# Two of the four output chunks of each attention output projection as Strassen products, in a two-layer decoder trunk on one core

## The chip, the core and the metric

The kernel runs on one core of one Trainium2 chip. The time is that of the device for one launch, in microseconds (us), as the median of several runs. TensorE (PE in the profile) does the matrix products, VectorE (DVE) and ScalarE (ACT) the work on single elements, GpSimd (POOL) a few masks, and SyncE (SP) issues nearly all transfers (DMA) between the chip's main memory and the core's on-chip memory.

## The reference

512 tokens of 2048 features pass two layers. Both layers end in the same way, and that end is what the change is about:

```python
def mixer(...):                      # attention of 16 heads of 128, sparse in layer 0, stick-breaking in layer 1
    return (o * jax.nn.silu(gate)) @ w_o            # output projection, 2048 x 2048

for i in range(DEPTH):                              # DEPTH = 2
    h = mixer(...)
    x = layer_norm(ALPHA * x + h, ln_g[i], ln_b[i]) # ALPHA = sqrt(2), over the 2048 features
    x = x + (p[i] @ w_ple[i]) * jax.nn.sigmoid(x @ w_ple_gate[i])
```

All is float32, and the outputs have to come out close to float32 accuracy.

## The kernel before

**Layout.** Activations lie with features on the 128 partitions and the 512 tokens along the free axis: a matrix of 2048 features is 16 blocks of 128 x 512. `F[0]` to `F[3]` (four blocks each, `fblock(n)` is block n) hold the running activations, `XH[k]` and `XL[k]` the two parts of block k when it is the operand of a projection.

**A product in three matmuls.** A float32 operand is split into a high part of reduced precision and the rest: `split` (L129) lets ACT write the high part and DVE the rest, so DVE always waits for ACT. `mm3` (L133) then issues three matmuls: high by high (L134), high weight by low activation (L135) and low weight by high activation (L136).

**Weights.** They are loaded as float32 in units of two row blocks (`raw`, three buffers, loaded by SP in the order of the list `units`), split into `wh` and `wl` (three buffers each, L224), and handed to TensorE two items ahead (`Ahead`, L203). An item is one row block of weights; its `wh` can be written only when TensorE is through with the item three before it. A plain product (`gemm_w`, L269) takes 16 items for a chunk of 512 output features, four `mm3` each, into four PSUM banks; with 256 features an item has two `mm3`.

**Strassen products.** Layer 1's shared keys, values and queries are already made this way (`strassen_items` L325, `gemm_s` L365, `combine` L388). A chunk of 512 output features becomes seven products of half the size in three dimensions: per item seven `mm3` on 256 tokens, 16 items to a chunk, into seven PSUM banks. On the side of the weights, DVE makes four sums `st` of each `raw` unit and splits them with ACT into `sh` and `sl` (three buffers each), beside `wh` and `wl` of 384 columns. On the side of the activations, `c3h` and `c3l` hold the split sums (`stream_sums`, L435), and the second half of the tokens in `XH[0..7]`, `XL[0..7]` is overwritten by one more sum, `t1` (`turn_first`, L448). `combine` puts a chunk together from its seven banks with three ACT copies and eight DVE sums.

**Order.** PE's order is the program's own order. ACT, DVE, POOL and SP each have one queue, in which instructions run strictly in order; a scheduler sets that order at build time. Side work (sums, squares, normalisation) stands in a list `bg` whose pieces `pumped` (L313) lets go between matmuls.

**The end of a layer** (`finish_layer`, L835). Before the change, all 2048 output features are plain products: three chunks of 512, then two of 256 (L892, L919). The residual is loaded over `F` by SP as soon as a part of `F` has been split (L901); DVE scales it and takes off a first estimate `cen` of the mean (`centred_residual`, L885), adds the projection out of PSUM (`onto`, L889), and gathers the sum `S` and the sum of squares `Qs` over the blocks (`moments`, L874). `total` (L857) sums over partitions with two matmuls: once in the second chunk, for `cen`, after nine items, and twice during `embed` (L965), the product of the per-layer embedding `p` that follows the projection. Before the last eight `mm3` steps, `pT` is loaded and split into `pth` and `ptl` (L947).

Of the kernel before, what the change touches and what calls it, by code (L numbers as in the profile page):

```python
# [10 lines left out]
F32 = mybir.dt.float32  # L11
# [66 lines left out]
def trunk_kernel(  # L78
# [42 lines left out]
    top = ctx.enter_context(tc.tile_pool(name="top", bufs=1))  # L121
    dram = ctx.enter_context(tc.tile_pool(name="dram", bufs=1, space=DRAM))
# [53 lines left out]

# [47 lines left out]
    def weight_parts():  # L224
        return tuple(top.tile([128, 512], F32R, name=n, tag=n, bufs=3) for n in ("wh", "wl"))
# [99 lines left out]
    def strassen_items(widths, wp):  # L325
        units = [n for n in widths for _ in range(NK // 2)]

        def prepare(n):
            raw = next_raw()
            rows = n // 256  # L330
            q = raw.rearrange("p a (b n) -> p (a b) n", b=2)
            two = [q[:, i].rearrange("p (j c) -> p j c", j=rows) for i in range(4)]
            st = wp.tile([128, 4 * H], F32, name="st", tag="st", bufs=2)[:, : 2 * n]
            st = st.rearrange("p (j i c) -> p j i c", j=rows, i=4)
            dve.tensor_tensor(st[:, :, 0], two[0], two[2], ALU.add)
            dve.tensor_tensor(st[:, :, 2], two[1], two[0], ALU.subtract)
            return q, two, st

        ready = prepare(units[0])
        for u, n in enumerate(units, 1):  # L340
            q, two, st = ready
            s1, s2, s3, s4 = (st[:, :, i] for i in range(4))
            dve.tensor_tensor(s2, s1, two[1], ALU.subtract)
            dve.tensor_tensor(s4, two[3], s2, ALU.subtract)
            rows = n // 256
            for j in range(rows):
                wh = top.tile([128, 512], F32R, name="wh", tag="wh", bufs=3)
                wl = top.tile([128, 512], F32R, name="wl", tag="wl", bufs=3)
                sh = wp.tile([128, 4, 128], F32R, name="sh", tag="sh", bufs=3)
                sl = wp.tile([128, 4, 128], F32R, name="sl", tag="sl", bufs=3)  # L350
                qh, ql = (w.rearrange("p (b c) -> p b c", b=4)[:, 0:3] for w in (wh, wl))
                split(qh, ql, q[:, 1:4, j * 128 : (j + 1) * 128])
                split(sh, sl, st[:, j])
                if j == rows - 1 and u < len(units):
                    ready = prepare(units[u])
                yield [(qh[:, i], ql[:, i]) for i in range(3)] + [(sh[:, i], sl[:, i]) for i in range(4)]

    def strassen_stream(widths, wp):
        return Ahead(strassen_items(widths, wp), 2)
# [28 lines left out]
    def combine(wp, M, dst):  # L388

        m1, m2, m6, m7, m5, m3, m4 = M  # L390
        u = wp.tile([128, 2, H], F32, name="u", tag="u", bufs=1)[:, : m1.shape[1]]
# [6 lines left out]
        dve.tensor_tensor(u, m6, u, ALU.add)  # L398
        pinned[0] = False

        def onto(c):
            dve.tensor_tensor(c, c, u, ALU.add)

        def rest():
            dve.tensor_tensor(c22, c12, c21, ALU.add)
            dve.tensor_tensor(c12, m3, c12, ALU.add)
            dve.tensor_tensor(c21, c21, m4, ALU.subtract)

        paced(rest)
        return [lambda c=c: onto(c) for c in (c12, c21, c22)]  # L410

    def combine_last(wp, M, dst):
# [6 lines left out]
        for out, a, b, op in (  # L419
            (c11, m2, u, ALU.add),  # L420
            (u, m6, u, ALU.add),
            (c21, m7, u, ALU.add),
            (c22, m5, c21, ALU.add),
            (c12, m5, u, ALU.add),
            (c12, m3, c12, ALU.add),
            (c21, c21, m4, ALU.subtract),
        ):
            dve.tensor_tensor(out, a, b, op)
# [19 lines left out]
    def turn_first(k, t1):  # L448

        split(XH[k][:, H:T], XL[k][:, H:T], t1)  # L450

# [45 lines left out]

    def add_finish(layer, w_o):
        add_parts(w_o, PARTS)
# [78 lines left out]
    iws = ip.tile([128, 3, 16], F32, name="iws")  # L578
    stacks = {}

    rc = ip.tile([128, 4], F32, name="rc")
    pool.dma_start(rc, rope_c)
# [750 lines left out]
```

## Time and profile before

| | |
|---|---|
| median of 3 runs | 1887.85 us (1887.64 to 1889.21) |
| span of the profiled execution | 1886.3 us |
| around it, against the median | 1.55 us |
| PE, DVE, ACT busy | 99%, 65%, 49% of the span |
| output projection of layer 0 | 620.5 to 795.6 us of the span |
| granted TensorE clock | full, in all slices |

A line of the page or of a view names the source line, the engine, the operation, and its tiles as out<-in; L111 is the helper through which nearly all ACT and DVE instructions are issued, so the tile names tell them apart. A matmul's row is longer than its share of the time, since matmuls overlap: the pace is the distance from one start to the next. The same holds, less strongly, for rows of DVE and ACT.

### The profile page before, as it was taken

What the parts mean: (1) busy time and instruction counts of PE and PEld (TensorE: products, weight loads), DVE (VectorE), ACT (ScalarE), POOL (GpSimd) and SP (SyncE); (2) the same over time, 40 slices, a digit from 0 to 9 for tenths busy, and PEclk for the clock granted to TensorE, in tenths of its full rate; (3) what the DMA queues carried; (4) which work ended last, traced back from release to release, by engine and by line L of the source; (5) the groups of instructions that cost most, each with busy time, mean ns of one, the idle gap of its engine ahead of it and who ended that gap; (6) DMA issues with size and microseconds to landing.
All of it is one profiled execution on the core that took longest, in us unless ns stands there. A gap on an engine that the chain in (4) does not pass through costs nothing.

```text
span 1886.3 us, 25050 instructions
## 1 busy us (share of the span) xinstructions
PE 1872.6 (99%) x9229; PEld 1586.7 (84%) x9229; DVE 1218.9 (65%) x2384; ACT 928.1 (49%) x1690; POOL 28.4 (2%) x49
## 2 busy tenths in 40 slices
PE   9999999999999999999999999999999999999998
PEld 8898888888888888888888999988888888888887
DVE  5668879966556454675368788866656645567534
ACT  4446323355554432474245444468877743347422
POOL 0000000000000000000000000000100000000000
PEclk9999999999999999999999999999999999999999
DMA  6432333312222432333343333322122153242333
GB/s 185 137 115 64 101 91 99 101 56 68 67 68 60 162 114 78 123 101 103 121 130 116 103 100 113 102 90 72 63 68 68 60 186 100 74 129 89 123 101 112
DMA packets 110587, 189.22 MB, mean 100 GB/s; under 512 B 8240, under 2 KB 28208, under 8 KB 110464
## 3 DMA queue, kind: packets, MB, share of 16 engines
q1 hardware_dynamic: 110320, 187.33, 32.4%
q8 instruction: 72, 1.18, 0.3%
q14 instruction: 51, 0.42, 0.1%
q0 software_dynamic: 144, 0.30, 0.1%
HBM read 179.21 MB, written 8.39 MB: 99 GB/s over the span
## 4 chain that ended last, share of the span: by engine, by line
PE 96%; DVE 2%; ACT 1%; DMA 1%; issue 0%; SPq 0%; POOL 0%; DVEq 0%; POOLq 0%
PE g L134 12%; PE g L135 12%; PE g L136 12%; PE o L135 7%; PE o L134 7%; PE o L136 7%; PE m L134 3%; PE m L135 3%; PE m L136 3%; PE q L136 3%; PE q L134 3%; PE q L135 3%; PE z L1214 2%; PE k L136 2%; PE k L135 2%; PE k L134 2%
## 5 line engine op out<-in xcount | busy, mean ns | idle before, releaser
L111 ACT ACTIVATE wh<-raw 128x512 fp32r<-128x512 f32 (+3 forms) x684 | 396.4, 581 | 674.4 <-PE g L135 239.4
L111 DVE TENSOR_TENSOR wl<-raw,wh 128x512 fp32r<-128x512 f32 (+3 forms) x684 | 429.6, 629 | 429.9 <-ACT wh L111 415.1
L134 PE MATMUL g<-xh,wh 128*128 128x512 f32 x1024 | 403.9, 394 | 0.2
L135 PE MATMUL g<-xl,wh 128*128 128x512 f32 x1024 | 400.3, 391 | 0.6 <-DVE xl L111 0.6
L136 PE MATMUL g<-xh,wl 128*128 128x512 f32 x1024 | 399.9, 390 | 0.0
L134 PEld LDWEIGHTS g<-xh,wh 128*128 128x128 f32 x1024 | 192.8, 188 | 40.4 <-ACT sg L111 1.9
L136 PEld LDWEIGHTS g<-xh,wl 128*128 128x128 f32 x1024 | 192.3, 188 | 40.8
L135 PEld LDWEIGHTS g<-xl,wh 128*128 128x128 f32 x1024 | 192.5, 188 | 38.4 <-DVE xl L111 1.4
L136 PE MATMUL o<-xh,wl 128*128 128x512 f32 x512 | 199.4, 389 | 0.1
L134 PE MATMUL o<-xh,wh 128*128 128x512 f32 x512 | 199.2, 389 | 0.0
L135 PE MATMUL o<-xl,wh 128*128 128x512 f32 x512 | 199.2, 389 | 0.0
L136 PEld LDWEIGHTS o<-xh,wl 128*128 128x128 f32 x512 | 96.1, 188 | 20.6 <-DVE wl L111 0.7
L134 PEld LDWEIGHTS o<-xh,wh 128*128 128x128 f32 x512 | 96.1, 188 | 20.2 <-ACT wh L111 0.2
L135 PEld LDWEIGHTS o<-xl,wh 128*128 128x128 f32 x512 | 96.1, 188 | 20.0
L134 PE MATMUL q<-xh,wh 128*128 128x512 f32 x256 | 99.6, 389 | 0.0
L135 PE MATMUL q<-xl,wh 128*128 128x512 f32 x256 | 99.6, 389 | 0.0
L136 PE MATMUL q<-xh,wl 128*128 128x512 f32 x256 | 99.6, 389 | 0.0
L111 ACT ACTIVATE sh<-st 128x512 fp32r<-128x512 f32 x80 | 49.0, 628 | 79.7 <-PE m L135 42.5
L111 DVE TENSOR_TENSOR sl<-st,sh 128x512 fp32r<-128x512 f32 x80 | 54.4, 689 | 37.2 <-ACT sh L111 37.2
L111 DVE TENSOR_TENSOR xl<-f,xh 128x512 fp32r<-128x512 f32 x80 | 54.3, 686 | 11.4 <-ACT f L111 11.0
L111 ACT ACTIVATE wk<-z 128x512 f32<-128x512 f32 x80 | 47.1, 590 | 25.7 <-PE z L136 18.0
L135 PEld LDWEIGHTS q<-xl,wh 128*128 128x128 f32 x256 | 48.1, 188 | 10.0
(290 smaller groups left out, 3366.5 us busy)
## 6 DMA issues: line engine op xcount, KB each, us to landing
raw<-w_in_a SPq DMA_DIRECT2D x95, 512.0 KB, 3.7
raw<-w_in_b SPq DMA_DIRECT2D x64, 512.0 KB, 3.8
raw<-w_ple_gate SPq DMA_DIRECT2D x52, 512.0 KB, 3.7
raw<-w_o_a SPq DMA_DIRECT2D x24, 512.0 KB, 3.9
raw<-w_o_b SPq DMA_DIRECT2D x24, 512.0 KB, 3.8
raw<-w_kv_b SPq DMA_DIRECT2D x16, 512.0 KB, 3.8
raw<-w_ple_gate SPq DMA_DIRECT2D x24, 256.0 KB, 2.9
f<-xT SPq DMA_DIRECT2D x4, 1024.0 KB, 6.4
```

The costliest lines, as they stand in the source:

```text
L111: ins = method(*args, **kw)
L134: pe.matmul(out, a[0], b[0], start=start, stop=False)
L135: pe.matmul(out, a[0], b[1], start=False, stop=False)
L136: pe.matmul(out, a[1], b[0], start=False, stop=stop)
L1214: pe.matmul(z, m, p, start=False, stop=n == len(terms), skip_group_check=True)
```

## The change

In both layers the output projection becomes: 512 features plain (here called stage A), 256 plain (B), chunks 2 and 3, that is blocks 8 to 15, as Strassen products (C2 and C3), and the remaining 256 features of chunk 1 plain (D). The embedding (E) follows as before.

- A and B use the rows of the activations in pairs (k, k + 8), and the four sums for Strassen are made beside them.
- The second token half of blocks 0 to 7, which `t1` overwrites, is stored to main memory before A (`late_halves`) and loaded and split again in D (`restore`).
- The attention output is scaled by 1/ALPHA where it is written, so the residual needs no factor; 1e-5 becomes 1e-5/ALPHA^2.
- ACT reads A's and B's banks out into `F`. The residual is then added by seven accumulating transfers that POOL issues (`add_residual`, 512 KB each), for 14 of the 16 blocks; for the last two it is loaded by SP and the projection is added by DVE.
- Taking off `cen` is one DVE instruction for two blocks (1024 elements a partition).
- `total` for `cen` stands after 11 items of B.
- Signs in the Strassen sums change for all Strassen products, with as many instructions as before. Some tiles get another size or place (`edge`, `iws`, `rc`, the descriptor memory).

PE has 9668 rows in the order after and 9092 before: 576 more, which is four chunks of 336 matmuls in place of four of 192.

Three places of the order, layer 0; layer 1 has the same rows. First, **ACT in the first chunk of 512**. Before, the high part `xh` of a block follows the `wh` of the item in front; `xh5` is used by item 5, and `wh_5649` is item 5's:

```order
L111 ACTIVATE wh_5631<-raw_5573 128x512
L111 ACTIVATE xh4_78<-f1_107 128x512
L111 ACTIVATE wh_5649<-raw_5573 128x512
L111 ACTIVATE xh5_79<-f1_107 128x512
L111 ACTIVATE wh_5670<-raw_5591 128x512
L111 ACTIVATE xh6_80<-f1_107 128x512
```

After, item 6 uses `xh3`, item 12 `xh6`; `wh_5723` is item 7's and `wh_5858` item 13's:

```order
L111 ACTIVATE wh_5707<-raw_5614 128x512
L111 ACTIVATE wh_5723<-raw_5614 128x512
L111 ACTIVATE c3h1_5568<-tf_5685 128x768
L111 ACTIVATE xh3_81<-f0_110 128x512
L111 ACTIVATE xh11_89<-f2_112 128x512
```

and, later in the same chunk:

```order
L111 ACTIVATE wh_5858<-raw_5750 128x512
L111 ACTIVATE xh7_85<-f1_111 128x512
L111 ACTIVATE xh15_93<-f3_113 128x512
L111 ACTIVATE c3h4_5574<-tf_5820 128x768
L111 ACTIVATE xh6_84<-f1_111 128x512
```

So the parts of one pair of blocks now stand behind a `wh` of a later item than the one that first uses them.

Second, **DVE ahead of the first `total`**, whose operand is `tl`. Before:

```order
L111 SCALAR_TENSOR_TENSOR f0_106<-f0_106,o0_5588 128x512
L111 TENSOR_TENSOR wl_5993<-raw_5900,wh_5992 128x512
L111 TENSOR_TENSOR S_5566<-S_5566,f0_106 128x512
L111 TENSOR_TENSOR tl_6062<-S_5566,th_6061 128x512
L111 TENSOR_TENSOR wl_6012<-raw_5936,wh_6011 128x512
```

After, with `wl_6079` item 11's, `wl_6093` item 12's and `wl_6113` item 13's; PE's first `total` matmul stands right behind item 10:

```order
L111 TENSOR_TENSOR S_5556<-f0_110 128x512
L111 TENSOR_TENSOR wl_6079<-raw_6013,wh_6078 128x256
L111 TENSOR_TENSOR xl1_95<-t11_5603,xh1_79 128x256
L111 TENSOR_TENSOR wl_6093<-raw_6041,wh_6092 128x256
L111 TENSOR_TENSOR S_5556<-S_5556,f0_110 128x512
L111 TENSOR_TENSOR xl2_96<-t12_5604,xh2_80 128x256
L111 TENSOR_TENSOR S_5556<-S_5556,f0_110 128x512
L111 TENSOR_TENSOR wl_6113<-raw_6041,wh_6112 128x256
L111 TENSOR_TENSOR st_6150<-raw_6090 128x256 x2
L111 TENSOR_TENSOR st_6150<-st_6150,raw_6090 128x256
L111 TENSOR_TENSOR tl_6107<-S_5556,th_6106 128x512
```

The three sums `S` now stand between the `wl` of items that come after `total`.

Third, **DVE at the end of the projection**. Before, the last weights are these (`wl_6854` and `wl_6864` belong to items 14 and 15 of the last 256 features):

```order
L111 TENSOR_TENSOR wl_6842<-raw_6785,wh_6841 128x256
L111 TENSOR_TENSOR ptl0_6876<-raw_6829,pth0_6875 128x512
L111 TENSOR_TENSOR ptl1_6880<-raw_6829,pth1_6879 128x512
L111 TENSOR_TENSOR wl_6854<-raw_6807,wh_6853 128x256
L111 TENSOR_TENSOR wl_6864<-raw_6807,wh_6863 128x256
```

After, from D's item 12 (`wl_7443`) to item 15 (`wl_7485`):

```order
L111 TENSOR_TENSOR wl_7443<-raw_7394,wh_7442 128x256
L111 TENSOR_TENSOR f3_113<-f3_113,cen_5558 128x1024
L111 TENSOR_TENSOR wl_7455<-raw_7394,wh_7454 128x256
L111 TENSOR_TENSOR S_5556<-S_5556,f3_113 128x512
L111 TENSOR_TENSOR Qs_5557<-Qs_5557,sq_7461 128x512
L111 TENSOR_TENSOR S_5556<-S_5556,f3_113 128x512
L111 TENSOR_TENSOR ptl0_7501<-raw_7440,pth0_7500 128x512
L111 TENSOR_TENSOR ptl1_7505<-raw_7440,pth1_7504 128x512
L111 TENSOR_TENSOR wl_7471<-raw_7418,wh_7470 128x256
L111 TENSOR_TENSOR Qs_5557<-Qs_5557,sq_7477 128x512
L111 TENSOR_TENSOR f3_113<-f3_113,cen_5558 128x1024
L111 TENSOR_TENSOR wl_7485<-raw_7418,wh_7484 128x256
```

Work on `F[3]`, which waits for its accumulating transfers, now stands among the last weights.

The core of the diff:

```diff
+    def restore(raw, k):
+        split(XH[k][:, H:T], XL[k][:, H:T], raw[:, k % 4])
...
     def add_finish(layer, w_o):
-        add_parts(w_o, PARTS)
+        for c0, n in ((0, 512), (512, 256), (1024, 512), (1536, 512)):
+            units.extend((w_o, k, k + 8, c0, n) for k in range(8))
+        rows = late_halves[layer].rearrange("(k p) t -> p k t", p=128)
+        for k in (8, 10, None, 12, None, 14, 0, 2, 4, 6):
...
+        def centre(c, j):
+            two = F[c][:, j : j + 2]
+            dve.tensor_tensor(two, two, cen[:, None].broadcast_to([128, 2, T]), ALU.subtract)
...
+        def add_residual(c, j):
+            pool.dma_start(F[c][:, j : j + 2], chunk_rows(resid, c)[:, j : j + 2], accum_op=ALU.add)
...
-        wo = plain_stream(*[(512, NK)] * 3, *[(256, NK)] * 2).prime()
+        def out_items():
+            yield from plain_items([(512, NK), (256, NK)])
+            yield from strassen_items(2, wp)
+            for first, n in ((0, 4), (4, 2)):
+                yield from plain_items([(256, n)])
+                raw = next_raw()
+                bg.extend(lambda raw=raw, k=k: restore(raw, k) for k in range(first, first + 4))
+            yield from plain_items([(256, 10)])
...
+        gemm = gemm_w(wo, plain, banks, order=PAIRS)
+        for k in range(8):
+            if k < 7:
+                paced(build_plain, k + 1)
...
+            steps(gemm, 5)
+            if k < 5:
+                bg.extend(stream_pieces(k))
...
+        for j, b in enumerate(banks):
+            paced(read_out, j, b)
+            if j % 2:
+                add_residual(0, j - 1)
+
+        banks = [bank(b, "o1") for b in (0, 1)]
+        gemm = pumped(gemm_w(wo, plain, banks, 256, order=PAIRS), 2)
+        bg.extend(piece for k in range(5, 8) for piece in stream_pieces(k))
+        steps(gemm, 14)
+        drain()
+        for n, t in zip((1, 2, 3), turns(range(3))):
+            bg.extend((t, lambda n=n: sum_block(n)))
+        steps(gemm, 8)
+        drain()
+        ps = total(parts_of(S), 3, gemm)
...
+        M = product_banks(2)
+        gemm = pumped(gemm_s(wo, C3, M), 5)
+        steps(gemm, 20)
+        bg.extend(moments(0, range(4)))
...
+        bg.extend(combine(lp, M, lambda i: quarter(F[2], i), "th"))
+        bg.extend(lambda j=j: add_residual(2, j) for j in (0, 2))
+        M = product_banks(1)
+        gemm = pumped(gemm_s(wo, C3, M), 4)
+        steps(gemm, 60)
+        bg.extend(moments(2, range(4)))
...
+        bg.extend(combine(lp, M, lambda i: quarter(F[3], i), "th"))
+        bg.extend(lambda j=j: add_residual(3, j) for j in (0, 2))
+        banks = [bank(b, "o3") for b in (0, 1)]
+        gemm = pumped(gemm_w(wo, plain, banks, 256, order=(*range(8, NK), *range(8))))
+        steps(gemm, 20)
+        bg.extend(moments(3, range(4)))
```

More of the change, by code (lines that the diff above doesn't have):

```diff
@@ L322, in drain, with strassen_items, prepare @@
             one()
[L325 to L348, printed above, removed]
+    def strassen_items(n, wp):
+        def prepare():
+            q = next_raw().rearrange("p a (b n) -> p (a b) n", b=2)
+            st = wp.tile([128, 4, 256], F32, name="st", tag="st", bufs=2)
+            dve.tensor_tensor(st[:, 0], q[:, 0], q[:, 2], ALU.add)
+            dve.tensor_tensor(st[:, 2], q[:, 1], q[:, 0], ALU.add)
+            return q, st
+        ready = prepare()
+        for u in range(n * NK // 2 - 1, -1, -1):
+            q, st = ready
+            dve.tensor_tensor(st[:, 1], st[:, 0], q[:, 1], ALU.add)
+            dve.tensor_tensor(st[:, 3], q[:, 3], st[:, 1], ALU.add)
+            for j in range(2):
+                wh, wl = weight_parts(384)
@@ L496, in add_parts @@
                 add_job(src, sum(parts[:i]), n)
+    late_halves = [dram.tile([8 * 128, H], F32, name=f"late{layer}") for layer in range(2)]
     def add_finish(layer, w_o):
-        add_parts(w_o, PARTS)
+        for c0, n in ((0, 512), (512, 256), (1024, 512), (1536, 512)):
+            units.extend((w_o, k, k + 8, c0, n) for k in range(8))
+        rows = late_halves[layer].rearrange("(k p) t -> p k t", p=128)
+        for k in (8, 10, None, 12, None, 14, 0, 2, 4, 6):
+            if k is None:
+                first = 4 * (units[-1][1] == 12)
+                units.append((rows[:, first : first + 4],))
+            else:
+                units.append((w_o, k, k + 1, 768, 256))
         add_job(pT[layer], 0, nk=2)
@@ L919, in gemm_part @@
-        def gemm_part(stream, c, n, where, every):
-            banks = [bank(b, f"o{c}") for b in where]
-            return banks, pumped(gemm_w(stream, plain, banks, n), every)
-        for c, where in ((1, (0, 1, 2, 3)), (2, (4, 5, 6, 7))):
-            banks, gemm = gemm_part(wo, c, 512, where, 3)
-            if c == 1:
-                steps(gemm, 36)
-                ps = total(parts_of(S), 7, gemm)
-                act.activation(cen, ps, AF.Copy, scale=-1.0 / 512.0)
-                bg.extend(lambda n=n: centre(n) for n in range(4))
-            bg.extend(lambda n=n: centred_residual(n) for n in range(4 * c, 4 * c + 4))
-            run(gemm)
-            drain()
-            for j, b in enumerate(banks):
-                bg.append(lambda n=4 * c + j, b=b: onto(n, b))
-                bg.append(lambda n=4 * c + j: moments(n))
@@ L937, in finish_layer, with read_out @@
-        banks, gemm = gemm_part(wo, 3, 256, (0, 1), 2)
-        bg.extend(lambda n=n: centred_residual(n) for n in range(12, 16))
+        def read_out(n, b):
+            act.activation(fblock(n), b, AF.Copy)
+        def out_items():
[6 more added lines that the diff above has]
+            yield from plain_items([(256, 10)])
```

181 lines of the change are left out of this document (100 added, 81 removed).

## The prediction

> **What bounds the kernel now.** I read the page's shares first, then the clock row and busy times by stretch, then the chain of waits, and last PE's, DVE's and ACT's timelines at the places that the change touches. From the page:
>
> ```profile
> PE 1872.6 (99%) x9229; PEld 1586.7 (84%) x9229; DVE 1218.9 (65%) x2384; ACT 928.1 (49%) x1690; POOL 28.4 (2%) x49
> PEclk9999999999999999999999999999999999999999
> ```
>
> PE is busy 99% of the 1886.3 us span, at full clock throughout. So only two things can move the time: how many matmuls there are and how long each takes, and how long PE waits. One stretch of plain output projection and one of Strassen products (columns: window, length, busy time and count of PE, PEld, DVE, ACT and POOL, clock, DMA share, GB/s):
>
> ```profile
> 620.00:660.00 40.00, 40.00 (x178) 33.12 (x177) 21.22 (x33) 18.47 (x33) 0.00 (x0) 1.00 0.55 181
> 1160.00:1200.00 40.00, 39.75 (x329) 39.35 (x328) 32.89 (x71) 17.17 (x33) 0.00 (x0) 1.00 0.36 106
> ```
>
> PE has no gap in the plain one. In the Strassen one DVE is busy 82% against 53%: the change puts load on the engine with less room, in the place where PE waits for nobody. PE's paces, from starts three matmuls apart:
>
> ```profile
> 620.48 0.39 PE L134 MATMUL o<-xh,wh 128*128 128x512 f32 x1
> 621.16 0.39 PE L134 MATMUL o<-xh,wh 128*128 128x512 f32 x1
> 1180.10 0.28 PE L135 MATMUL m<-xl,wh 128*128 128x256 f32 x1
> 1180.46 0.28 PE L135 MATMUL m<-c3l,sh 128*128 128x256 f32 x1
> ```
>
> 0.68 / 3 = 0.227 us for 512 tokens, 0.36 / 3 = 0.120 for 256.
>
> **PE's own work: −6.4 us a layer.** A plain chunk has 192 matmuls, 43.5 us by the pace; a Strassen chunk 336, 40.3 us. Per layer two replace two: 87.0 − 80.6 = 6.4 us, 12.8 in all. The sevenths saved (12.5%) shrink to 7.4% because the half-length matmul costs 53% of the long one. [...] The trace shows 0.227 and 0.120, so the measured paces stand.
>
> What PE loses must be set against 6.4.
>
> **Change-over between Strassen chunks: +0.9.** The chain passes the same step of three successive chunks of shared weights:
>
> ```profile
> 1117.04 0.58 ACT sh L111
> 1158.43 0.64 ACT sh L111
> 1199.50 0.64 ACT sh L111
> ```
>
> The periods are 41.39 and 41.07 us, 0.9 on the mean above 40.3. The banks of one chunk are read out while the next waits for them, which the view of waits shows only in part (us, count, mean):
>
> ```profile
> PE m L134 <- DVE f L111: 0.4, 2, 0.2
> ```
>
> C3 follows C2 in the same way, so I take 0.9; the ends are 0.4 (only that wait) and 1.1 (41.39 − 40.3).
>
> **Prices of DVE and ACT.** Rows overlap by some 0.1 us, so starts count where instructions queue:
>
> ```profile
> 1160.84 0.68 DVE L111 TENSOR_TENSOR f<-m,u 128x512 f32<-128x512 f32 x1
> 1161.44 0.41 DVE L111 TENSOR_TENSOR st<-st,raw 128x256 f32<-128x256 f32 x1
> 1161.77 0.68 DVE L111 TENSOR_TENSOR u<-m,u 128x512 f32<-128x512 f32 x1
> L111 DVE TENSOR_TENSOR c3l<-E,c3h 128x768 fp32r<-128x768 f32 x8 | 7.6, 953 | 0.4 <-ACT c3h L111 0.3
> L111 ACT ACTIVATE wh<-raw 128x256 fp32r<-128x256 f32 x112 | 46.5, 417 | 99.3 <-PE o L135 53.3 <-PE g L135 39.7 <-ACT sq L111 3.5
> ```
>
> On DVE 512 elements take 0.60, 256 take 0.33 to 0.34, 768 some 0.87 (0.953 less the overlap); I estimate 1024 at 1.14, two rows of 512 less an overlap. From the first item of A to the total in B this makes DVE busy 148.6 us over the whole projection, against 167.7 us of PE's own (174.2 − 6.4): enough on average. So what matters is order, not load.
>
> **A: +0.85 and +1.0.** A high part `wh` needs its buffer, which PE frees three items back. The same situation stands in layer 1's keys:
>
> ```profile
> 993.64 0.39 PE L134 MATMUL k<-xh,wh 128*128 128x512 f32 x1
> 1004.54 0.63 ACT L111 ACTIVATE wh<-raw 128x512 fp32r<-128x512 f32 x1 [2.14 <-PE k L135]
> 1005.08 0.83 ACT L111 ACTIVATE c3h<-E 128x768 fp32r<-128x768 f32 x1
> 1005.82 0.40 ACT L111 ACTIVATE xh<-E 128x256 fp32r<-128x256 f32 x1
> ```
>
> An item of 512 features is 12 matmuls, 2.72 us; 1004.54 is 993.64 plus four items, and this `wh` is the seventh item's. In the new order `xh3`, wanted by item 6, stands behind item 7's `wh`, which waits until item 4 is done, 5 × 2.72 = 13.6 us into A. ACT reaches `xh3` in time, but DVE has to do, after `wh` (0.63), that item's `wl` (0.60), three pieces of 256 (0.33 each), `c3l1` (0.87) and `xl3` (0.69): ready at 17.4. Item 6 wants `xl3` for its second matmul at 6 × 2.72 + 0.23 = 16.55, so PE waits 0.85. In the same way DVE does behind item 13's `wh` (free at 11 × 2.72 = 29.9) `wl`, `xl7`, `xl15`, `c3l4` and `xl6` in turn: ready at 29.9 + 0.63 + 3 × 0.60 + 0.87 + 0.69 = 33.9, wanted at 12 × 2.72 + 0.23 = 32.9: 1.0. The lower end is 0, since each wait is less than the two or three pieces that the count puts ahead; the upper 3.7, if a row of 768 more (0.87) stands in each.
>
> **B: +2.1.** `total`'s first matmul stands behind item 10, 11 × 1.36 = 15.0 us in. DVE's last sum `S` stands behind the `wl` of item 12, whose buffer comes free at 13.6. Then 0.42 (`wh`) + 0.34 (`wl`) + 0.60 + 0.34 + 0.69 gives 16.0, and ACT's `th` 16.6: PE waits 1.6. Behind that matmul it does one `mm3` (0.9 together) and wants `tl`, which stands behind item 13's `wl` and three weight sums: 16.0 + 0.34 + 1.0 + 0.69 = 18.0 against 17.5, 0.5 more. Ends: 0.5 and 2.6 (if a weight load is half a microsecond late).
>
> **D: +0.6.** The trace has this place of before:
>
> ```profile
> 786.44 4.34 DMA raw<-pT
> 790.81 0.64 ACT pth L111
> 791.47 1.29 DVE L111 TENSOR_TENSOR ptl<-raw,pth 128x512 fp32r<-128x512 f32 x2 [2.34 <-ACT pth L111]
> 792.68 0.75 DVE L111 TENSOR_TENSOR wl<-raw,wh 128x256 fp32r<-128x256 f32 x2
> 792.65 0.40 PE L135 MATMUL o<-xl,wh 128*128 128x512 f32 x1
> 793.15 0.50 PE L136 MATMUL o<-xh,wl 128*128 128x512 f32 x1
> ```
>
> `pT` takes 4.34 us from a buffer that comes free late, `ptl` follows, and `wl` behind it reaches PE 0.27 late (0.50 where the pace is 0.227). The new order has the same chain, freed by item 11's `wl` at 9 × 1.36 + 0.42 + 0.34 = 13.0 us into D: 17.3 landed, 18.0 `pth`, 19.2 `ptl`, 19.6 item 14's `wl` (wanted 19.5). Then `Qs` and a 1024-wide subtraction stand ahead of item 15's `wl`: 21.7 against 20.95, so 0.85 in all, 0.6 more than now. Ends: 0 and 1.7.
>
> **E: +0.9.** Behind item 15's `wl` one `centre`, two sums `S` and a split stand ahead of the first total in the embedding: an estimated 1.14 + 1.2 + 1.3 = 3.6 us, against 12 matmuls of product, 2.7 us, that PE has until then. Ends 0 and 2.
>
> **At nothing.** The late halves are stored and loaded again on SP's queue among the weights, 512 KB at a time; a Strassen chunk needs 512 KB per two items (5 us of PE), as the 106 GB/s of the stretch in layer 1 already show, and a plain one runs at 181 GB/s today. ACT's read-outs replace DVE's `onto` on the same banks, ACT being busy 49%. POOL, which issues the residual, is busy 2%. If the cover of a load fails, that load costs at most its 3.9 us.
>
> **The accumulating transfers: 0 taken, ends 0 and +11.5 a layer.** The trace shows none. Nearest rows (KB each, us to landing):
>
> ```profile
> raw<-w_o_a SPq DMA_DIRECT2D x24, 512.0 KB, 3.9
> raw<-w_o_a SPq DMA_DIRECT2D x16, 256.0 KB, 2.9
> f<-xT SPq DMA_DIRECT2D x4, 1024.0 KB, 6.4
> lnc<-ln_c POOLq DMA_DIRECT2D x1, 32.0 KB, 3.0
> posi<-pos POOLq DMA_DIRECT2D x1, 256.0 KB, 5.5
> ```
>
> The tight place is D: both halves of `F[3]` are issued from about 3.2 us in, and DVE's first `centre` on them, in the queue ahead of the last `wl`s, can be 14.7 late without harm. A fixed 3.0 us (32 KB on POOL's queue), then per 512 KB 2.0 (2.9 to 3.9) to 2.5 us (3.9 to 6.4) plain. An accumulation also reads its target, so I double: 4.0 each, both through at 3.2 + 3.0 + 8.0 = 14.2. I take this, hence 0, but it is free by half a microsecond only. The 256 KB row on POOL's own queue argues the other way: 2.5 us more for 224 KB is 5.7 for 512 KB plain, though it repeats one row of memory for 128 partitions while the start-up loads run. [...]
>
> **Sum.** Per layer −6.4 + 0.9 + 0.85 + 1.0 + 2.1 + 0.6 + 0.9 = −0.05. Twice that is −0.1: span 1886.2. The median stands 1.55 above the span, so the predicted time is some 1888 us, no change. Its own range: half of the smaller waits gone (−4) to a little over them (+4), 1884 to 1892.
>
> **Rivals.**
>
> *Faster: ACT and DVE arrive in time.* The waits of A and B are differences of about one instruction's length between two times counted over 15 to 30 us; if the queues run ahead there, only 0.9 + 0.6 + 0.9 remain. For it: PE waited for almost nothing in the same projection of before. Against it: `wh` can't be written earlier than its buffer is free. Per layer −6.4 + 2.4 = −4.0: 1887.85 − 8.0 = 1880. Without any but the change-over it would be 1877.
>
> *Slower: DVE held by the accumulating transfers.* DVE's queue is strict, so a `centre` waiting for `F[3]` holds the weights of items 13 to 15 behind it, and PE stops; in B the same happens behind `F[0]`. With 5.0 us per 512 KB both halves are through at 16.2 in place of 14.2, 1.5 late: +3 in all, 1891. From about 5.2 us per 512 KB it decides, being slower by over 0.2% (3.8 us, about what a measurement of this kernel can tell from no change). At 7.5, three times plain, D waits 6.5 and B 2.9 per layer: 1888 + 19 = 1907. At the 10 that doubling 5.0 would make, D waits 11.5. For it: the POOL row of 5.5 us. Against it: the plain 512 KB rows.
>
> *The saving is not there.* If the 256-token pace in C2 and C3 were 0.130 instead of 0.120, as with weights late at every item, all 6.4 would go and the time would be near 1901. Layer 1 runs the same inner loop at 0.120 today, with DVE's same sums, so this is counted within the slower cases.
>
> **How the numbers follow.** I give no change 0.40, the faster rival 0.32, and the slower ones 0.28, as the waits are worked out one by one, and each could be off by its own size in either direction. The likeliest is no change, so the time is 1888.0. The faster case is wholly in down to 1878; of the slower cases I leave out what is above 1898, about half of them (0.14), and below 1878 some 0.05. The three chances are those of the three cases.
>
> **What would show it.** Right: two chunks near 41 us each in C2 and C3; PE gaps of about 1 us before `xl3` and `xl6` of A, 1.6 us before the total of B. Wrong: no gap there and the end of the projection earlier by over 4 us; or a gap on PE in D released by a DVE instruction that waits for an accumulating transfer into `f`, with landing times above 8 us for the first half.

## The result, and the profile after

The change makes the kernel slower: 1912.45 us (median of 4 runs, 1910.83 to 1914.67) against 1888.32 us for the kernel before; the ratio is 1.0127, with a 95% interval of 1.0112 to 1.0141. The forecast was no change.

The page's lines that answer to those of before:

```profile
PE 1871.8 (98%) x9805; PEld 1608.7 (84%) x9805; DVE 1332.2 (70%) x2676; ACT 988.6 (52%) x1826; POOL 45.8 (2%) x63
PEclk9999999999999999999999999999999999999999
q1 hardware_dynamic: 110864, 184.18, 31.4%
q0 software_dynamic: 3952, 7.64, 2.4%
```

PE is busy some 1 us less than before and the span is 1912.6 us in place of 1886.3: the time is in waits, and in matmuls that run slower after them. (The busy time of a matmul row, 0.39 us at a pace of 0.227, includes its overlap and, below, a slower clock, so this share says little about the saving.) The stages as stretches, first those of layer 0 (A and B, C2 and C3, D, E), then two pieces of D. The columns are those of the prediction, with the clock and the DMA share ahead of GB/s:

```profile
619.98:695.78 75.80, 69.62 (x291) 55.92 (x290) 53.04 (x109) 40.24 (x75) 2.45 (x2) 0.95 0.40 103
695.78:779.11 83.33, 81.85 (x673) 80.90 (x672) 75.44 (x152) 41.30 (x80) 3.58 (x3) 1.00 0.46 116
779.11:809.61 30.50, 24.73 (x99) 19.56 (x98) 18.66 (x39) 12.69 (x31) 2.43 (x2) 0.89 0.58 153
809.61:833.29 23.68, 23.20 (x101) 18.62 (x100) 19.91 (x33) 18.05 (x31) 0.00 (x0) 1.00 0.33 111
786.00:793.40 7.40, 1.99 (x8) 1.38 (x7) 0.54 (x2) 0.99 (x4) 0.00 (x0) 0.84 0.85 166
793.40:797.80 4.40, 4.40 (x12) 3.37 (x11) 2.49 (x8) 1.99 (x7) 0.00 (x0) 0.50 0.37 122
```

Against 65.3, 80.6 and 21.8 us by the paces, A and B lose 10.5, C2 and C3 2.7, D 8.7. The last row, a piece of D, can't be seen in the 40 slices of the page: after a wait PE is busy without a gap for 4.4 us at a granted clock of 0.50.

PE's waits, sorted by releaser (us in total, times, longest):

```profile
PE o L135 <- ACT wh L111: 10.2, 3, 5.4
PE sum L864 <- DVE tl L111: 5.3, 2, 2.7
PE sum L862 <- ACT th L111: 4.8, 4, 1.9
PE o L136 <- DVE xl L111: 2.8, 4, 0.8
```

The last three are waits of A and B that were forecast, the one on `tl` at 0.5 us a layer. The first, the largest, was not forecast. It is D's: counted from one start to the next, less the pace, PE stands still for 5.6 us in layer 0 and 4.1 in layer 1. The chain of waits shows what stands behind it:

```profile
784.39 0.34 DVE wl L111
784.75 7.55 DMA raw<-w_o_a
792.41 0.42 ACT wh L111
792.88 0.79 PE o L135
793.67 0.43 PE o L136
...
797.51 0.43 PE o L136
797.94 0.24 PE o L137
```

256 KB of weights take 7.55 us where the rows of before had 2.9, and after that PE's pace is 0.43 us instead of 0.227 for ten matmuls, called half pace from here on. The view of transfers names the neighbours:

```profile
f<-xT POOLq DMA_DIRECT2D x7, 512.0 KB, 7.9
f<-x POOLq DMA_DIRECT2D x7, 512.0 KB, 7.4
raw<-w_o_a SPq DMA_DIRECT2D x16, 256.0 KB, 3.3
```

POOL issued the two halves of `F[3]`'s residual at the moment when that load was due:

```profile
783.41 2.43 POOL L889 DMA_DIRECT2D f<-xT  x2 [37.60 <-DVE f L111]
```

In the view of waits no row of DVE names an accumulating transfer. In B the chain has the same shape: a load, sums of Strassen weights, and only then the operand of the total:

```profile
680.07 5.08 DMA raw<-w_o_a
685.14 0.02 issue
685.17 1.10 DVE st L111 x3
686.26 0.61 DVE tl L111
686.88 0.04 issue
686.92 0.80 PE sum L864
```

The lengths of the stages in the runs that the text compares most, from PE's first matmul of each stage (us; layer 0, layer 1):

| kernel | A + B | C2 + C3 | D | E | median us |
|---|---|---|---|---|---|
| by the paces; E as before | 65.3 | 80.6 | 21.8 | 23.3 | |
| after | 75.8, 75.2 | 83.3, 81.3 | 30.5, 30.0 | 23.7, 23.7 | 1912.45 |
| no residual | 74.7, 74.2 | 81.1, 81.1 | 26.5, 25.5 | 23.7, 23.7 | 1902.51 |
| no reload of late halves | 75.9, 75.3 | 82.2, 81.5 | 25.0, 24.5 | 23.7, 23.7 | 1901.62 |
| late half early | 75.1, 75.3 | 82.4, 81.5 | 26.9, 26.6 | 23.5, 23.7 | 1907.73 |
| sums first, total later | 69.2, 69.6 | 85.9, 85.8 | 29.0, 29.1 | 23.7, 23.7 | 1908.92 |
| sums first alone | 71.6, 71.8 | 83.0, 81.8 | 29.1, 30.0 | 23.7, 23.7 | 1905.86 |
| floor | 68.4, 68.0 | 81.7, 81.6 | 22.5, 23.4 | 23.7, 23.7 | 1884.65 |
| joined | 69.5, 69.0 | 84.3, 86.1 | 22.9, 23.4 | 23.7, 23.7 | 1894.47 |

Before, A to D took 175.1 and 174.7 us as plain products and E 23.3.

### The profile page after: what moved, and what is told of

It is laid out like the page before. It is cut to its first block, busy times and chain, and to the rows that moved or that the text cites. A ratio compares the mean times of both kernels' runs of the same rounds, so it can differ in the third digit from the quotient of the medians.

```text
span 1912.6 us, 26741 instructions
## 1 busy us (share of the span) xinstructions
PE 1871.8 (98%) x9805; PEld 1608.7 (84%) x9805; DVE 1332.2 (70%) x2676; ACT 988.6 (52%) x1826; POOL 45.8 (2%) x63
## 3 DMA queue, kind: packets, MB, share of 16 engines
q0 software_dynamic: 3952, 7.64, 2.4%
## 4 chain that ended last, share of the span: by engine, by line
PE 90%; DVE 4%; DMA 3%; ACT 1%; issue 1%; SPq 0%; POOL 0%; DVEq 0%; ACTq 0%; POOLq 0%
PE g L135 12%; PE g L136 12%; PE g L137 12%; PE m L135 5%; PE m L137 5%; PE m L136 5%; PE o L136 3%; PE o L135 3%; PE o L137 3%; PE q L136 3%; PE q L137 3%; PE q L135 3%; PE k L137 2%; PE k L136 2%; PE k L135 2%; PE z L1271 2%
## 5 line engine op out<-in xcount | busy, mean ns | idle before, releaser
L136 PE MATMUL g<-xl,wh 128*128 128x512 f32 x1024 | 400.3, 391 | 0.7 <-DVE xl L111 0.7
L136 PEld LDWEIGHTS g<-xl,wh 128*128 128x128 f32 x1024 | 192.8, 188 | 38.0 <-DVE xl L111 1.5
L111 DVE TENSOR_TENSOR sl<-st,sh 128x512 fp32r<-128x512 f32 x144 | 98.0, 689 | 39.2 <-ACT sh L111 39.2
L135 PE MATMUL o<-xh,wh 128*128 128x512 f32 x256 | 103.7, 405 | 10.4 <-ACT wh L111 10.2
L136 PE MATMUL o<-xl,wh 128*128 128x512 f32 x256 | 103.5, 404 | 2.8 <-DVE xl L111 2.8
L137 PE MATMUL o<-xh,wl 128*128 128x512 f32 x256 | 103.0, 402 | 0.9 <-DVE wl L111 0.8
L136 PE MATMUL q<-xl,wh 128*128 128x512 f32 x256 | 99.7, 390 | 0.0
L137 PE MATMUL m<-xh,wl 128*128 128x256 f32 x288 | 82.1, 285 | 1.3 <-DVE wl L111 1.1
L135 PE MATMUL m<-c3h,sh 128*128 128x256 f32 x288 | 82.2, 285 | 0.2
L135 PE MATMUL m<-xh,sh 128*128 128x256 f32 x288 | 81.8, 284 | 0.0
L135 PE MATMUL m<-xh,wh 128*128 128x256 f32 x288 | 81.7, 284 | 0.0
L136 PE MATMUL m<-c3l,sh 128*128 128x256 f32 x288 | 81.6, 283 | 0.0
L136 PE MATMUL m<-xl,sh 128*128 128x256 f32 x288 | 81.6, 283 | 0.0
```

What stands on the lines that cost most here:

```text
L111: ins = method(*args, **kw)
L135: pe.matmul(out, a[0], b[0], start=start, stop=False)
L136: pe.matmul(out, a[0], b[1], start=False, stop=False)
L137: pe.matmul(out, a[1], b[0], start=False, stop=stop)
```

## The experiments

The kernel before ran beside each group, at 1888.3 to 1888.6 us. Times are medians; the edits are against the changed kernel. Theory T: transfers hold up the loads of weights. Theory O: the order of queues and buffers does. Theory R: DVE waits for the accumulating transfers, as the prediction's slower rival had it.

**1. Without the residual's transfers.**

```diff
         def add_residual(c, j):
-            pool.dma_start(F[c][:, j : j + 2], chunk_rows(resid, c)[:, j : j + 2], accum_op=ALU.add)
+            return
```

> The residual of 14 blocks is left out: POOL issues none of the seven accumulating transfers of a layer, everything else stays. Theory T (the accumulating transfers hold up the loads of weights, 7.6 us for 256 KB where D's wait of 5.6 and 4.1 us stands, and a long wait is followed by ten matmuls at 0.427 us): the load at D falls to about 3 us, D's first wait to about 1 us, B's two waits (2.1 and 2.9) to what the order of the sums S makes, 1.6 and 0.5; no half pace; about 9 us a layer come back, 1894 us. Theory O (the order alone: loads issued late because the late halves hold buffers, sums S behind later weights): D's first wait stays over 3.5 us, B's over 4, time above 1905. Theory R (DVE waits for the accumulating transfers): the time falls as by T, but the waits of the changed kernel would name DVE behind such a transfer.

1902.51 us, 9.9 less. D is 4.0 and 4.5 us shorter and has no half pace. The load in D, from the chain of waits:

```profile
781.25 0.34 DVE wl L111
781.59 0.03 DVE xl L111
781.62 3.75 DMA raw<-w_o_a
```

Half of 7.55 us goes with the neighbours: T holds for D. But the load is still issued only when the second `wl` of the weights before it has freed a buffer (at 781.59; the `xl` of 0.03 us is only next in DVE's queue), and D still waits 1.8 and 1.2 us in layer 0; and B keeps waits of 1.8 and 2.0 us with half pace behind them. The time lies between the two expected: less than half of the loss is the accumulating transfers. R isn't told apart by the time; the waits of the changed kernel, above, speak against it.

**2. The same transfers, written over instead of added.**

```diff
-chunk_rows(resid, c)[:, j : j + 2], accum_op=ALU.add)
+chunk_rows(resid, c)[:, j : j + 2])
```

> The same seven transfers of a layer with the same bytes on POOL's queue, but written over the target in place of added to it (the projection is lost in 14 blocks). If the addition is what makes them slow and heavy (T with the price in the accumulation): they land in about 5 us in place of 7.4 to 7.9, the weights beside them in 4 us, and half of the loss in B and D comes back, about 1902 us. If what counts is 512 KB pieces of another queue among the weights, or the order: landing and time as in the changed kernel, 1910 to 1914 us.

1909.61 us, 2.8 less (intervals 1.0096 to 1.0127 against 1.0112 to 1.0141: just overlapping). The rows:

```profile
f<-xT POOLq DMA_DIRECT2D x7, 512.0 KB, 5.5
f<-x POOLq DMA_DIRECT2D x7, 512.0 KB, 5.1
q0 software_dynamic: 2160, 7.64, 1.2%
```

The queue's packets take 1.2% of the engines' time where accumulating ones took 2.4%, for the same 7.64 MB: here adding cost twice the engine time, as the prediction assumed, and 2.3 to 2.4 us per landing. D's wait only falls from 5.6 to 4.8 us in layer 0 and the half pace stays, for the load beside them is still slow:

```profile
780.85 6.75 DMA raw<-w_o_a
```

That is 6.75 us beside plain transfers, 7.55 beside accumulating ones and 3.75 beside none, so in layer 0 the larger part of the delay is there with plain transfers too. The gain of 10 us expected was too much.

**3. Idle matmuls in D's wait.**

```diff
-        steps(gemm, 20)
+        steps(gemm, 12)
+        warm = bank(2, "warm")
+        for _ in range(16):
+            pe.matmul(warm, neg, XH[8], start=True, stop=True)
+        steps(gemm, 8)
         bg.extend(moments(3, range(4)))
```

> 16 matmuls of 512 tokens without use, 3.6 us, stand in D between items 5 and 6, where PE waits 5.6 us in layer 0 and 4.1 in layer 1; nothing else changes. If the half pace after that wait (ten matmuls 0.427 us apart, 2.0 us lost) comes from PE having stood still: matmuls after it run at 0.227 again, 2 us a layer come back, 1908 to 1909 us. If it comes from something else (late operands, transfers): the half pace stays and the time is 1912, or up to 1913 if the idle matmuls hold PE beyond the wait.

1915.15 us, no gain. The load came no sooner, so in layer 0 PE still stood still after the idle matmuls:

```profile
786.67 3.79 PE L994 MATMUL warm<-xh,neg 128*128 128x512 f32 x16
792.80 0.50 PE L135 MATMUL o<-xh,wh 128*128 128x512 f32 x1 [2.34 <-ACT wh L111]
...
793.83 0.59 PE L136 MATMUL o<-xl,wh 128*128 128x512 f32 x1
794.21 0.63 PE L137 MATMUL o<-xh,wl 128*128 128x512 f32 x1
```

Half pace followed again, some 1.1 us after the wait, at a granted clock of 0.51. In layer 1, where the wait left was 1.6 us, none followed and D was 0.8 us shorter. The two projections together are 0.5 us shorter in the profile; 2.0 us are lost in layer 1's mixer, which the edit doesn't touch (the last section says how). Whether matmuls that fill the whole wait would keep the clock stays open; here 2.5 us without work were followed by half pace.

**4. Late halves one load later.**

```diff
-        for k in (8, 10, None, 12, None, 14, 0, 2, 4, 6):
+        for k in (8, 10, 12, None, 14, None, 0, 2, 4, 6):
```

> In D each load of a late half is issued one load of weights later (8, 10, 12, late, 14, late instead of 8, 10, late, 12, late, 14), so the weights of items 6 and 7 no longer wait for the third buffer until a late half has been split. Theory O: they are issued 2.8 us earlier, ahead of the accumulating transfers, D's first wait of 5.6 and 4.1 us falls under 2.5, with no half pace after it: 4 to 5 us a layer less, 1903 us. Theory T alone: the transfers then hold up the next loads instead, the wait moves to item 8 and is as long, 1909 to 1913 us.

1917.46 us: not better, 5 us worse by the medians (intervals 1.0139 to 1.0173 against 1.0112 to 1.0141, just overlapping). The wait moved to item 8 and was 6.0 and 5.6 us long. PE waited there for `wh`, the item's weights, and not for a late half: these weights now stood behind it and took 8.62 us. D itself is 0.8 and 1.0 us shorter, but E's first total waits 2.0 us in both layers (E 25.2 us in place of 23.7). The two profiled spans differ by only 1.0 us, so where the 5 us lie isn't shown. O's time fails; T had the wait right and its price too low.

**5. Sums S first, total later.**

```diff
-        for n, t in zip((1, 2, 3), turns(range(3))):
-            bg.extend((t, lambda n=n: sum_block(n)))
-        steps(gemm, 8)
+        bg.extend(lambda n=n: sum_block(n) for n in (1, 2, 3))
+        bg.extend(turns(range(3)))
+        steps(gemm, 14)
```

> In B the three sums S stand together ahead of the first three turned halves, and the total stands three items later (14 in place of 11). Theory O for B (the split of S stands on DVE behind sums of weights whose load can't start before item 11 is split): both waits in B and the half pace after them go, 2.1 + 2.9 + 0.4 + 1.4 to 2.0 us, about 7 us a layer, 1898 us. Theory T for B (transfers hold up what DVE needs): the wait moves on to the first Strassen items, which need the same load, and less than 3 us a layer come back, over 1906 us.

1908.92 us, 3.5 less instead of 14. A and B fall by 6.6 and 5.6 us, as expected of O, but C2 and C3 rise by 2.6 and 4.5. PE's waits now name Strassen's weights:

```profile
PE m L137 <- DVE wl L111: 4.5, 4, 1.8
```

The load that the total waited for comes no sooner, and C2 needs it next.

**6. Without the reload.**

```diff
-        for k in (8, 10, None, 12, None, 14, 0, 2, 4, 6):
+        for k in (8, 10, 12, 14, 0, 2, 4, 6):
...
-            for first, n in ((0, 4), (4, 2)):
-                yield from plain_items([(256, n)])
-                raw = next_raw()
-                bg.extend(lambda raw=raw, k=k: restore(raw, k) for k in range(first, first + 4))
-            yield from plain_items([(256, 10)])
+            yield from plain_items([(256, NK)])
```

> The late halves are still stored, but not loaded and split again in D, so D multiplies the turned halves in eight blocks (a wrong operand, the same work on PE). D then loads 2 MB of weights in place of 3 MB, and no third of the buffers is held. If the reload is half of what D waits for: no wait over 1.5 us in D and no half pace, 7 to 8 us a layer less, 1897 us. If the accumulating transfers alone fill the queues: D's first wait stays over 3 us, the time over 1906 us.

1901.62 us, 10.8 less. D's first wait is 0.6 us in layer 0 and 0.8 in layer 1, without half pace. But the load beside the accumulating transfers is as slow as ever:

```profile
785.13 8.33 DMA raw<-w_o_a
793.46 0.02 issue
793.48 0.04 ACTq L111
```

So D's long wait needs two things at once: a load that is issued late, because late halves hold the other buffers, and a load that is slow, because the residual is on the way. Taking away either gives back 4 to 5.5 us a layer there; the two gains don't add.

**7. One late half in C3.**

```diff
+        units.insert(-1, (rows[:, 0:4],))
-        for k in (8, 10, None, 12, None, 14, 0, 2, 4, 6):
+        for k in (8, 10, 12, None, 14, 0, 2, 4, 6):
...
-            yield from strassen_items(2, wp)
+            for i, item in enumerate(strassen_items(2, wp)):
+                if i == 27:
+                    raw = next_raw()
+                    bg.extend(lambda raw=raw, k=k: restore(raw, k) for k in range(4))
+                yield item
```

> The first late half is loaded in C3, ahead of its last unit of weights, and split there; the second stays in D behind 8, 10 and 12. All work is kept. By what the shift of one load showed (the wait moved from item 6 to item 8, the first that needs a late half), D's wait should now go with the load that caused it: 1.5 us or less, no half pace, 6 to 7 us a layer less, 1899 us. Rival: C3, where DVE is busiest, gets eight more instructions and its weights come late, or the accumulating transfers hold up whatever load stands next: the wait moves again and is as long, 1907 to 1914 us.

1907.73 us, 4.7 less: D 26.9 and 26.6 us, C2 and C3 hardly touched. The rival about C3 fails. The other one, that the transfers hold up whatever load stands next, holds in part: the wait moved on to item 10, in layer 0 behind a load of 8.68 us, and is shorter, 2.5 and 2.0 us, with half pace after it. The 1899 us expected were not reached; the time is in the rival's range. (The expectation calls item 8 of run 4 the first that needs a late half; it waited for its weights.)

**8. A's parts a pair earlier.**

```diff
         paced(build_plain, 0)
+        paced(build_plain, 1)
...
-            if k < 7:
-                paced(build_plain, k + 1)
+            if k < 6:
+                paced(build_plain, k + 2)
```

> In A the two parts of each pair of blocks are made one pair earlier. Theory (order, as in the prediction: they stand behind a weight of a later item): A's waits of 1.0, 0.3 and 0.9 us go, 2.1 us a layer, 1908 us. Rival: the work ahead of A (the gate's sigmoids on ACT) is held up by the same two instructions more, and PE waits there: 1911 to 1914 us.

1907.91 us, 4.5 less; the row "PE o L136 <- DVE xl" of 2.8 us is gone. A's waits were order, of the forecast size.

**9. The residual of chunk 3 loaded plainly in C3.**

```diff
+            if c == 3:
+                dve.tensor_tensor(two, two, res3[:, j : j + 2], ALU.add)
+                return
...
-        steps(gemm, 60)
...
+        res3 = tp.tile([128, 4, T], F32, name="res3")
+        steps(gemm, 40)
+        for j in (0, 2):
+            paced(dve.memset, res3[:, j : j + 2, 0:2], 0.0)
+            nc.sync.dma_start(res3[:, j : j + 2], chunk_rows(resid, 3)[:, j : j + 2])
...
-        bg.extend(lambda j=j: add_residual(3, j) for j in (0, 2))
```

> The residual of chunk 3 no longer comes by two accumulating transfers in D: SP loads it in C3 into memory that A and B have left, DVE takes cen off it there (two instructions of 1024 more in C3) and adds it in D in the place where it took off cen. All else stays. Theory T for D (the accumulating transfers hold up the loads of weights): D gets as short as without any residual, 26.5 and 25.5 us in place of 30.5 and 30.0, no half pace, 8 us less in all, 1904 us. Rival (any 1 MB more beside the weights costs as much, or DVE in C3 has no room): C3 gets longer by what D gets shorter, 1909 to 1913 us.

1909.18 us, 3.3 less: the rival's range. D gains 2.9 and 5.1 us, but C3 gets waits on `wl` of up to 1.9 us, its weights standing behind 1 MB on SP's queue; C2 and C3 together are 4.0 us longer in layer 1 and as long as before the edit in layer 0.

**10. Edits 5, 7 and 8 joined.**

> The three edits that kept the reference's output are joined: parts of a pair made earlier in A, sums S first and the total later in B, the first late half loaded in C3. Alone they gave 4.5, 3.5 and 4.7 us; if their causes are separate places, 1899.7 us. If they share one cause (loads that are late on average, so that a wait gone in one place returns in the next): over 1903 us.

1899.29 us, 13.2 less, where the single gains add to 12.7: separate places.

**11. These, edit 9, and `F[1]`'s half residual put off into C2.**

> The three edits, the plain load of chunk 3's residual as above, and the load of half of F[1]'s residual on SP's queue put off from B until the 20th step of C2, away from the first Strassen weights. From 1899.7: D loses its last long wait (26.8 to some 23.5 us), the start of C2 1.5 of 3.4 us a layer: 1890 us, at best 1886. If DMA or DVE is full over the whole stage: no better than the three edits, 1898 us or more.

1895.16 us. D is 22.8 and 23.3 us, 1.0 and 1.5 above the paces, but C2 and C3 are 88.1 and 87.5.

**12. Edits 5 and 8, no residual, no reload.**

> The edits of A and B, and no transfer that the change added in the projection but the stores of the late halves: the residual of 14 blocks is left out, and the late halves are neither loaded nor split again (wrong operands, the same work on PE). What is left is order. If the waits that B's edit moved into C2 (0.7 and 1.8 us, with 1.1 at B's end) come from DVE's order (sums of the first Strassen unit, which wait for its load, ahead of B's last weights): they stay, 1885 to 1888 us. If the added transfers cause them: they go, and 1888 - 12.8 plus about 2.5 us a layer gives 1880 us.

1886.80 us, as expected if the waits come from order. With none of these transfers the waits at the turn to C2 stay:

```profile
PE m L137 <- DVE wl L111: 4.0, 4, 1.4
```

So the transfers don't cause them. That DVE's order does is what is left, and argued; the next two runs try it.

**13 and 14. The first Strassen sums behind B's last weights on DVE**, in run 12 and in run 11, the latter with its two loads of chunk 3's residual apart.

```diff
-        ready = prepare()
+        with tc.issue_after(behind.ins):
+            ready = prepare()
```

> As the run before, with the first sums of Strassen weights put behind the last weights of B on DVE. If order causes the waits at the turn from B to C2: 3 us a layer less than the run before, 1880 us. If not: the same time as the run before.

> All work kept: the version without accumulation in D, with the first sums of Strassen weights behind B's last weights, and the two plain loads of chunk 3's residual 20 steps of C3 apart in place of together. From 1895 us: 2 to 3 us a layer at the turn to C2 if order causes that, 1 us in C3 where the weights stood behind 1 MB: 1888 us, no faster than before the change. If the waits move on once more: 1893 to 1896 us.

1888.42 and 1896.73 us, no gain in either. The wait changed its name:

```profile
PE m L137 <- ACT cen L111: 3.2, 2, 1.6
```

`cen` is read from a PSUM bank that C2's second product needs; it now stands on ACT behind the Strassen sums, and these behind their load. A wait of 1.9 us follows in both layers of both runs, with half pace behind it in three of the four places. So that this order was the cause isn't shown.

**15. Sums first, total where the change has it.** Edit 5 without its last line.

> As the run in which the sums S stood first, but the total stays after 11 items, where the change has it. On DVE its operand now stands ahead of the first sums of Strassen weights, and cen is known three items earlier than in that run. If B's waits are order: the first falls from 2.1 to under 0.5 us, the second from 2.9 to under 0.7, no half pace, and C2 keeps its 40 to 41 us, since the centring isn't crowded: 6 to 7 us a layer less, 1899 us. If the load of the first Strassen unit sets the end of B whatever the order: the wait moves to C2 as it did there, 1907 to 1910 us.

1905.86 us, 6.6 less. The waits of B's total nearly go, as O expected (first row; the second is the new wait at B's end):

```profile
PE sum L862 <- ACT th L111: 2.1, 4, 0.6
PE o L137 <- DVE wl L111: 2.7, 4, 1.0
```

The wait on `tl` falls from 2.9 to 0.2 us and there is no half pace in B; but of the 7 us a layer expected, A and B gain only 4.2 and 3.4, since B's last items now wait 0.7 and 1.0 us (0.7 and 1.2 in layer 1) for weights behind the Strassen load.

**16. Edits 15 and 8, no residual, no reload (floor).**

> That order of B, A's parts a pair earlier, and neither the residual of 14 blocks nor the reload of the late halves (wrong operands, the same work on PE). If the forecast saving of 6.4 us a layer is there and only order and the added transfers eat it: 1888 - 12.8 and about 2 us a layer for the turns between chunks, pT and the totals, 1879 us. If a Strassen chunk in this place costs more than in layer 1's keys and values: 1885 us or more.

1884.65 us, ratio 0.9981 (0.9972 to 0.9990). With part of the work left out this is 3.6 us under before, not 9. C2 and C3 took 81.7 and 81.6 us, so the saving of matmuls is there; A and B still lose 3.1 and 2.7 us, most of it at the turn to C2, the Strassen chunks 1.0, D 0.7 and 1.6, E 0.35. The load at B's end is as slow as in the changed kernel, where it took 5.08 us, so that length isn't the added transfers':

```profile
680.34 5.22 DMA raw<-w_o_a
```

**17 and 18. All work kept, joined:** edits 15, 7, 8 and 9 with `F[1]` put off; then with the residual in pieces of 256 KB, the order of run 14 and the total in bank 7.

> All work kept: the sums S first with the total after 11 items, A's parts a pair earlier, the first late half loaded in C3, chunk 3's residual loaded plainly in C3, half of F[1]'s residual put off into C2. A and B 66.3, C2 and C3 84, D 23, the embedding 23.7 us make 197 a layer against 198.2 before: 1885 us, the first to beat the kernel before. If the waits of B move on into C2: 1892 to 1896 us.

> As the joined version (1894.5 us), with all plain residual loads in pieces of 256 KB, each at least 24 matmul steps from the next, the first sums of Strassen weights behind B's last weights on DVE, and the first total in another bank, which C2 needs later. If 512 KB amid the weights is what makes C2 and C3 lose some 1 us per load (5 waits of 0.9 to 1.2 us in layer 1), 256 KB pieces stay hidden: C2 and C3 82.5 in place of 84.3 and 86.1; the turn from B to C2 loses 1 us less: 1888 us. If bytes count and not pieces, or the waits at the turn move on again: 1892 to 1895 us.

1894.47 and 1892.67 us (ratio of the last 1.0020, 1.0011 to 1.0029): still slower than before. In C3 of the last one PE waits 1.9 us while DVE is busy throughout and no transfer runs, and half pace follows (stretches of its trace):

```profile
767.90:769.80 1.90, 0.26 (x3) 0.05 (x1) 1.90 (x6) 0.60 (x2) 0.00 (x0) 1.00 0.00 0
771.40:774.70 3.30, 3.30 (x19) 3.30 (x17) 3.07 (x6) 2.88 (x7) 0.00 (x0) 0.51 0.54 177
```

Yet it isn't for want of time on DVE: just before, DVE had stood idle for 2.34 us until a load of weights landed, and then a centring stands ahead of the `wl` that PE waits for:

```profile
767.50 0.76 DVE L111 TENSOR_TENSOR st<-raw 128x256 f32<-128x256 f32 x2 [2.34 <-DMA raw<-w_o_a]
768.18 1.22 DVE L111 TENSOR_TENSOR f<-f,cen 128x1024 f32<-128x1024 f32 x1
```

It is the chain of B and D once more, a late load and the order behind it. In layer 1 no wait on `wl` in C3 is over 0.6 us. The last run's three edits together help by less than the runs can tell (1.0011 to 1.0029 against 1.0021 to 1.0045).

## Why the prediction was wrong

**PE's own work, −6.4 a layer: not refuted.** C2 and C3 took 81.1 us without the residual, 0.5 over the pace of 0.120 us; the rival's 0.130 would be 87.

**A, 1.85 forecast, 2.45 measured; change-over and E, 0.9 each, 0.5 to 2.7 and 0.35 measured.** A took 45.97 us in both layers against 43.52 before, with gaps of 0.97 and 0.88 us at the two places named. Run 8, where A takes 43.52 again, shows that the cause was the one named. The faster rival, in which ACT and DVE arrive in time, fails.

**B, 2.1 forecast, 8.1 and 7.5 measured: the second wait was mis-sized, and half pace had no term.** The first wait was near (2.1 for 1.6). For the second the prediction counted the three sums of Strassen weights ahead of `tl` as 1.0 us of work and put half a microsecond on a late load. But the load can't be issued before item 11's `wl` has freed a buffer, at 680.07, 14.1 us into B; with the 3.9 us of the rows it lands at 18.0 and `tl` follows at 19.7, 2.2 late for the 17.5 of the prediction. It took 5.08 us, and about as long without the added transfers (5.22, run 16). The rows for a late issue were all there; the step that failed is that the sums' input was taken as present. Half pace (1.4 to 2.0 us) came on top.

**D, 0.85 in all forecast, 8.5: "at nothing" failed.** It said that a load whose cover fails costs at most its 3.9 us. The step that failed is that the reload and its neighbours cost nothing; the runs showed a chain in its place: buffers held by late halves, a load issued late, a transfer slowed to 7.55 us, and half pace after it. The waits forecast at `pT` came, 0.5 us in layer 0 and 1.0 and 0.6 in layer 1.

**The accumulating transfers: the sum right, the payer wrong.** Doubling the plain price was right by engine time (2.4% against 1.2%, run 2). The prediction had both halves of D through 11.0 us after the first was issued; in layer 0 they landed 6.4 and 10.5 us after their issues, the second 11.3 after the first's. DVE didn't wait for them. The slower rival had the sign and nearly the size (1907), but by luck, by a mechanism that no row shows: it asked who waits for the transfers, not whose transfers share the engines with them (busy to 0.85 from 786.0 to 793.4 us). They cost 9.9 us; in the profile of run 1 the two D stages give back 8.6, through the loads of weights.

**Half pace: no term.** 10 + 10 matmuls in layer 0 and 7 + 8 in layer 1 at 0.427 in place of 0.227 us are 7.0 us. The trace of before holds one such case, four matmuls after a wait of 3.9 us in layer 1's mixer, which the prediction didn't look for; it called the clock full throughout.

Of the 24 us, removed one by one: A's order 4.5, B's order 6.6, residual 9.9, reload 10.8; these sum to 31.8, and all together gave 27.8, as the last two share D's wait. What DVE's order at the turn to C2 could still give with all work kept is open: two orders were run, and each made another wait.

## What to carry to other kernels

Where PE is the bound, cost a change by the loads that it puts off as well as by the instructions that it adds: for each operand ask when its buffer comes free, who loads beside it, and what stands behind it in the queue. A reload needs both a buffer and a place among the loads; in D of layer 0 PE waited 1.8 us with a load issued late but not slow (run 1), 0.6 with one slow but not late (run 6), and 5.6 with both together. And a wait on PE can cost more than its length by the clock: in the projections of the changed kernel seven to ten matmuls at half pace, 1.4 to 2.0 us, followed waits of 2.9 to 5.6 us.

## What the runs showed of the hardware

Half pace came in pieces of 3.41 or 6.83 us. The granted clock of the changed kernel around D's wait (columns as above):

```profile
787.60:791.00 3.40, 0.00 (x0) 0.00 (x0) 0.00 (x0) 0.00 (x0) 0.00 (x0) 1.00 0.89 189
791.00:797.80 6.80, 4.92 (x12) 3.87 (x13) 3.03 (x9) 2.98 (x9) 0.00 (x0) 0.50 0.52 129
797.80:801.20 3.40, 3.40 (x16) 2.80 (x15) 1.02 (x3) 1.25 (x3) 0.00 (x0) 1.00 0.48 154
```

The clock fell inside the wait, 1.9 us before PE had work again, and rose 6.8 us later under work. In all 20 traces the clock record holds 0.50 for 3.41 or 6.83 us at a time (start-up and end apart), and within a trace these pieces start on a grid of 3.41 us (in the changed kernel at 685.18, 791.00, 1279.10, 1586.30 and 1692.12 us). Cut into such windows, by PE's starts and paces, the trace of the changed kernel has five at full clock in which PE stood still for 2.07, 2.38, 2.42, 3.19 and 3.41 us in sum, and half clock followed each; it followed none of the others before the end, with at most 1.64 us. Counted over all 20 traces, half clock followed all 57 such windows with more than 2.05 us, none with less than 1.98 us, and four of six between.

So in these runs a wait of some 2 us cost something or nothing by how it fell on the grid. Single waits of 1.92 to 1.97 us were enough in three runs (1.94 in C3 of run 18), two of 2.0 us in E of run 4 were not; waits of 0.6 and 1.9 us close together were enough in layer 0 of run 13, not in layer 1 of run 14. The mixer of layer 1 has a wait of 3.9 us in every trace. In the changed kernel and its variants the stretch with this mixer, from the end of layer 0's E to layer 1's A, took 688.7 to 689.2 us where 3.41 us at half clock followed, and 689.9 to 691.1 where 6.83 did: some 1 to 2 us, in a place that no edit touches.

An accumulating transfer of 512 KB landed 7.4 to 7.9 us after its issue (medians), the same bytes plain on the same queue 5.1 to 5.5; a plain load of 512 KB of weights on SP's queue 3.7 to 3.9 in the kernel before. The loads of 256 KB that PE waited for in D took 5.8 to 8.8 us beside two accumulating transfers (7.55 and 6.04 in the changed kernel, 8.62 in run 4, 8.68 in run 7), 6.75 and 5.25 beside two plain ones, 3.75 without them.
